# A hybrid mLSTM and GDN block: odd heads' first phases one piece later, one decay load moved, and the gate's sigmoid in the mLSTM's own stage

## The chip, the core and the metric

The kernel runs on one core of a Trainium2 chip. The metric is the device time of one execution in microseconds (us). A core has five engines with a queue each: TensorE (PE) for matmuls, VectorE (DVE), ScalarE (ACT), GpSimd (POOL) and SyncE (SP). Each engine works its queue in order. SP, POOL and ACT also issue DMA transfers.

## The reference

One layer of a bidirectional encoder, for 256 tokens of width 2048 in float32. A first matrix product of c gives shifts, scales and gates (ada); a second projects the normed input h to the inputs of two branches and of their merge:

```python
proj = h @ w_in
# branch A, mLSTM, 4 heads: q, k of 256, v and output gate o of 512
h_a = bidirectional(mlstm_chunkwise, (q_a, k_a, v_a), ...)
y_a = (jax.nn.sigmoid(a_o) * rms_norm(h_a)) @ w_branch_a
# branch B, GDN (gated delta rule), 16 heads of 128
o_b = bidirectional(gated_delta_chunkwise, (q_b, k_b, v_b), ...)
y_b = (rms_norm(o_b) * jax.nn.silu(b_z)) @ w_branch_b
x = x + gate_m * ((g_a * y_a + g_b * y_b) @ w_out)
# then a SwiGLU feed-forward of width 5632, and a final RMSNorm
```

The gated delta rule needs, for each head, the inverse of a unit triangular matrix; the mLSTM needs row sums of its decayed scores for its denominator. The output gate is the sigmoid of a_o.

## The kernel before

**Matmuls.** The large products are made of float32 operands split in two (fp32r): the weights come as tiles of 1 MB (`raw`), ScalarE copies half a tile to `wh` (L182, L209) and VectorE subtracts to get `wl` (L184, L211); TensorE then makes three matmuls for each block. Half a tile's matmuls are a *piece*: in `tjob` 12 matmuls over 512 columns (L230 to L232), in `fjob` 24 matmuls over 256 columns (L187 to L189). The pool of `raw` has three buffers, and wh and wl have three each. The ada rows, also 1 MB each, share the `raw` buffers; VectorE sums each of them (L111).

**Jobs.** A weight tile is named after its job. b8_2 is the third projection of GDN head 8 (j = 0, 1, 2: k, q and v; the v part ends in `vf`, a silu on ScalarE at L337). z0 to z3 are the gates of the four groups of GDN heads. v, o, a and m jobs (o = output gate; ma and mb = merge gates; a = q and k of the mLSTM) make up the list `fills`: work that nothing near it waits for. `fill(n)` puts n pieces of it into the program.

**GDN.** 16 heads in 4 groups of 4. `gdn_phase1(h)` has two steps. The first makes the decay scans, and on TensorE the transposes of vf (`vps`, L601) and the sums of squares (L603). The second makes square roots (L611), products k k and q k (`ks`, L630), the matrices mi and mb, and ends with POOL's DMAs: four stores to `inst_d` (L651), the load of the decays of head h + 2 (`decay_load`, a memset at L312 and a DMA at L313), and the load of a part of `uu` (L658). `gdn_invert(g)` then solves for the group's inverses on VectorE; it begins with a memset (L687) that waits for the last load of uu, and yields to a fill piece every few steps. `gdn_phase2(g, p)` works off two heads p of group g; its last step (`px`, L829) transposes the result, ScalarE scales it into `obt` (L833) and stores it to `ob_d` (L834).

**What sets the order.** The program is written out in one order for all engines. While the two heads of a pair run phase 2, `stream(h0)` puts in the b jobs of two heads of the next group (6 pieces for each head), and then fill pieces; each of these pieces counts down the list `todo`. An entry `[n, h]` runs the next step of head h's phase 1 when n more pieces have been put in. After a head's last b piece the entries `[2, h]` and `[4, h]` are added. Then a group's last pair goes on taking pieces until its second head is done, the job z of the next group is put ahead of the fills, and the group's solve begins.

**The mLSTM's head.** Behind the last px the GDN's memory is given back, and the mLSTM's heads 0 and 1 go on: `pden` (L950, row sums by matmuls of one column), `dn` (L952, its absolute value, in the memory that the GDN's had), the loads of the four parts of ob_d (`o4`, L1066, two buffers), `ph` (L966, the numerators, in the four PSUM buffers that pden also uses), their eviction into hs with dn as the scale (L968, L969), and a square with sum (L970). `o_split` cuts o4 into `obh` (L1070) and `obl` (L1071), the operands of the branch product `yb`. The output gate `sgo` comes back from o_d by POOL's DMA (L939). What is left of `fills` is put in by fill(1), fill(2) and fill(1000) among these steps; the yb job is what follows.

Of the kernel before, what the change touches and what calls it, by code (L numbers as in the profile page):

```python
# [11 lines left out]
AF = mybir.ActivationFunctionType  # L12
# [9 lines left out]
NH_B, DK_B = 16, 128  # L22
# [3 lines left out]
GRP = 4  # L26
# [26 lines left out]
def hybrid_block(ctx: ExitStack, tc: tile.TileContext, xr, nfr, crow, pk_d, cst_d, ada2, ada4, win0, winb, wint, wba, wbb, wo, wgu, wd, out, dbg=None):  # L53
    nc = tc.nc
    V, S, G, PE = nc.vector, nc.scalar, nc.gpsimd, nc.tensor
# [228 lines left out]
    v_d = [tc.dram_tile([P, 2, 512], F32, name=f"v_d{h}") for h in range(NH_A)]  # L284
    o_d = [tc.dram_tile([P, 2, 512], F32, name=f"o_d{h}") for h in range(NH_A)]
# [24 lines left out]
    def decay_load(h):  # L310
        al = als[h] = fr.tile([P, 2, T + 8], F32, tag="al", bufs=2, name=f"al{h}")
        order(G.memset(al[:, :, 0:8], 0.0))  # L312
        order(G.dma_start(al[:, :, 8:], alpha_d[:, h].partition_broadcast(P)))  # L313
# [32 lines left out]
    def keep(dst, fn, name):  # L346

        def done(ps):
            ev = evp.tile([P, 2, 512], F32, tag="ev", bufs=2, name=f"ev_{name}")
            for t in range(2):  # L350
                S.activation(ev[:, t], ps[t], fn)
            S.dma_start(dst, ev)
        return done
# [21 lines left out]
    def a_vo(i, h):  # L375
        return tjob(
            f"{'vo'[i]}{h}", [wint[4 + 4 * i + h, u] for u in range(4)], hh, hl,
            keep((v_d, o_d)[i][h], (AF.Copy, AF.Sigmoid)[i], f"{'vo'[i]}{h}"),
        )

    def m_job(i, g):
# [201 lines left out]
    def gdn_phase1(h):  # L583
# [62 lines left out]
        g, hl_ = divmod(h, GRP)  # L646
# [5 lines left out]
                inst[4 * b : 4 * b + 4].rearrange("x j i -> j x i"), mi[32 * b : 32 * b + 32, :, 32 * b : 32 * b + 32]  # L652
            ), b)

        final = hl_ == GRP - 1
        if h + 2 < NH_B and not final:
            decay_load(h + 2)
        order(G.dma_start(uus[g][16 * hl_ : 16 * hl_ + 16], inst))  # L658
        if h + 2 < NH_B and final:
            decay_load(h + 2)  # L660

        cc = ccs[h % NB]

# [211 lines left out]
    def stream(h0):  # L875

        todo = []

        def piece():

            for q in list(todo):
                q[0] -= 1
                if not q[0]:
                    todo.remove(q)
                    next(heads1[q[1]])

        for h in range(h0, min(h0 + 2, NH_B)):
            for j in range(3):
                for _ in b_job(h, j):
                    piece()  # L890
                    yield True
            todo += [[2, h], [4, h]]
        while todo:
            fill(1)
            piece()
            yield True
        while True:
            fill(1)
            yield True
# [3 lines left out]
    def mlstm(h):  # L903
# [34 lines left out]
        so = ml.tile([P, 2, DV_A], F32, tag="so", bufs=2, name=f"sgo{h}")  # L938
# [21 lines left out]
        for t in range(2):  # L960
            pn = []
            for d in range(2):
                ph = gps(f"ph{h}_{t}_{d}")
                terms = src[d, t]
                for i, (w, s) in enumerate(terms):
                    PE.matmul(ph, w, vt[:, s], start=i == 0, stop=i == len(terms) - 1)  # L966
                pn.append(ph)
            S.activation(hs[:, t], pn[0], AF.Copy, scale=dn[:, t, 0:1])  # L968
            V.scalar_tensor_tensor(hs[:, t], pn[1], dn[:, t, 1:2], hs[:, t], ALU.mult, ALU.add)  # L969
            S.activation(sq, hs[:, t], AF.Square, accum_out=ss[:, t : t + 1])  # L970
            yield
        S.activation(ss, ss, AF.Sqrt, bias=epsc, scale=1.0 / DV_A)
        V.reciprocal(ss, ss)
        for t in range(2):
# [2 lines left out]
        for e2 in range(2):  # L977
            px = gps(f"pxa{h}_{e2}")
            for e in range(2):
                f = 2 * e2 + e  # L980
# [25 lines left out]
    def invert(g):  # L1006
        gen = gdn_invert(g)
        next(gen)
        fill(4 if g else 6)
        for _ in gen:  # L1010
            fill(1)

    invert(0)
# [365 lines left out]
    for j in range(FB // 4):  # L1379
# [4 lines left out]
        for e2 in range(2):  # L1384
            px = gps(f"pxf{j}_{e2}")
            for e in range(2):
                f = 2 * e2 + e
# [154 lines left out]
```

## Time and profile before

| what | value |
| --- | --- |
| three runs | 2049.5, 2056.79 and 2057.14 us, median 2056.79 us |
| the profiled execution | 2056.26 us |
| its span, from the first instruction to the last | 2054.3 us |
| mean granted TensorE clock | 0.992 |
| GDN stage (from the second group's b jobs to the last px) | 323 to 983 us of the span |
| head of the mLSTM | 983 to about 1115 us |

All times in the text are microseconds from the start of the span. A row of the timeline gives the start, the duration, the engine, the line of the kernel, the operation, the tile written, the tiles read, and in brackets how long the engine stood idle ahead of it and what it waited for; xN is a group of N instructions. A row of the windows view gives a stretch's length, the busy time of each engine in it with the number of instructions, the granted TensorE clock as a part of 1, the share of DMA in use, and GB/s. A matmul of float32 that isn't split stands as two records.

### The profile page before, as it was taken

How to read it: one execution, taken by the hardware profiler on the slowest of the kernel's cores; microseconds unless marked ns; L12 is line 12 of the kernel's file. 1: busy time of each engine (PE TensorE's matmuls, PEld its weight loads, DVE VectorE, ACT ScalarE, POOL GpSimd, SP SyncE). 2: the span in 40 equal slices, each digit the busy share in tenths (PEclk: the TensorE clock that was granted, in tenths of full speed). 3: DMA queues.
4: the chain of work that ended last, by engine and by line, in shares of the span. 5: the costliest groups of instructions: out<-in, count | busy, mean ns of one | idle time of the engine just before them, and what ended most of it. 6: DMA issues, size and time to landing. Idle time of an engine off the chain costs nothing.

```text
span 2054.3 us, 27025 instructions
## 1 busy us (share of the span) xinstructions
PE 2017.2 (98%) x10386; PEld 1698.6 (83%) x10386; DVE 1397.7 (68%) x2062; ACT 1027.4 (50%) x1541; POOL 116.6 (6%) x211
## 2 busy tenths in 40 slices
PE   8999999999999999999999999999999999999998
PEld 6878789988997888889787888788888888878886
DVE  5778877877888788866577778756556554555554
ACT  3146647765675667455534444644444444444443
POOL 0001210111011010100100000200000000000000
PEclk9999999999999999999999999999999999999999
DMA  9986666656666666686776877466666665555553
GB/s 400 420 332 209 195 224 227 220 165 212 226 199 221 245 205 226 205 288 260 260 269 254 309 292 289 163 236 237 237 226 234 254 226 187 193 194 196 193 192 136
DMA packets 78962, 485.64 MB, mean 236 GB/s; under 512 B 10585, under 2 KB 15969, under 8 KB 24433
## 3 DMA queue, kind: packets, MB, share of 16 engines
q1 hardware_dynamic: 63216, 450.69, 60.5%
q0 software_dynamic: 8160, 17.88, 3.9%
q10 hardware_dynamic: 7458, 15.36, 2.0%
q8 instruction: 81, 1.33, 0.3%
q14 instruction: 47, 0.39, 0.1%
HBM read 467.07 MB, written 16.82 MB: 236 GB/s over the span
## 4 chain that ended last, share of the span: by engine, by line
PE 86%; DMA 6%; DVE 5%; ACT 1%; issue 1%; POOL 0%; ACTq 0%; SPq 0%; DVEq 0%; POOLq 0%
PE acc_gt L230 4%; PE acc_gt L232 4%; PE acc_gt L231 4%; PE acc_up L232 4%; PE acc_up L231 4%; PE acc_up L230 4%; PE acc_d L230 4%; PE acc_d L232 4%; PE acc_d L231 4%; DMA ra<-ada 3%; PE acc_o L232 3%; PE acc_o L230 3%; PE acc_o L231 3%; PE acc_b L187 2%; PE acc_b L188 2%; PE acc_b L189 2%
## 5 line engine op out<-in xcount | busy, mean ns | idle before, releaser
L211 DVE TENSOR_TENSOR wl_d<-raw_d,wh_d 128x1024 fp32r<-128x1024 f32 x88 | 107.9, 1226 | 119.9 <-ACT wh_d L209 119.9
L211 DVE TENSOR_TENSOR wl_up<-raw_up,wh_up 128x1024 fp32r<-128x1024 f32 x88 | 107.8, 1226 | 111.9 <-ACT wh_up L209 111.9
L211 DVE TENSOR_TENSOR wl_gt<-raw_gt,wh_gt 128x1024 fp32r<-128x1024 f32 x88 | 108.6, 1234 | 89.1 <-ACT wh_gt L209 89.1
L187 PE MATMUL acc_b<-hh,wh_b 128*128 128x256 f32 x576 | 164.7, 286 | 0.0
L209 ACT ACTIVATE wh_d<-raw_d 128x1024 fp32r<-128x1024 f32 x88 | 93.3, 1061 | 139.0 <-PE acc_d L231 134.0
L189 PE MATMUL acc_b<-hh,wl_b 128*128 128x256 f32 x576 | 160.8, 279 | 0.0
L188 PE MATMUL acc_b<-hl,wh_b 128*128 128x256 f32 x576 | 159.6, 277 | 0.0
L209 ACT ACTIVATE wh_gt<-raw_gt 128x1024 fp32r<-128x1024 f32 x88 | 93.3, 1060 | 128.7 <-PE acc_gt L231 77.3
L111 DVE SCALAR_TENSOR_TENSOR ada<-ada,crow 128x2048 f32<-128x2048 f32 x64 | 146.2, 2284 | 10.8 <-DMA ada<-ada 10.8
L209 ACT ACTIVATE wh_up<-raw_up 128x1024 fp32r<-128x1024 f32 x88 | 93.2, 1060 | 118.0 <-PE acc_up L231 84.2
L230 PE MATMUL acc_gt<-wh_gt,hfh 128*128 128x512 f32 x352 | 139.2, 395 | 0.1
L231 PE MATMUL acc_gt<-wh_gt,hfl 128*128 128x512 f32 x352 | 138.3, 393 | 0.0
L232 PE MATMUL acc_gt<-wl_gt,hfh 128*128 128x512 f32 x352 | 137.5, 391 | 0.0
L230 PE MATMUL acc_up<-wh_up,hfh 128*128 128x512 f32 x352 | 136.9, 389 | 0.0
L231 PE MATMUL acc_up<-wh_up,hfl 128*128 128x512 f32 x352 | 136.9, 389 | 0.0
L232 PE MATMUL acc_up<-wl_up,hfh 128*128 128x512 f32 x352 | 136.9, 389 | 0.0
L230 PE MATMUL acc_d<-wh_d,ffh 128*128 128x512 f32 x344 | 134.3, 391 | 0.0
L231 PE MATMUL acc_d<-wh_d,ffl 128*128 128x512 f32 x344 | 134.3, 390 | 0.0
L232 PE MATMUL acc_d<-wl_d,ffh 128*128 128x512 f32 x344 | 133.9, 389 | 0.0
L557 PE MATMUL first<-x,raw 128*128 128x256 f32 x512 | 115.9, 386 | 6.4 <-ACT x L551 6.4
L557 PEld LDWEIGHTS first<-x,raw 128*128 128x128 f32 x512 | 97.3, 192 | 25.1 <-ACT x L551 12.0
L187 PEld LDWEIGHTS acc_b<-hh,wh_b 128*128 128x128 f32 x576 | 108.4, 188 | 1.2 <-issue 0.9
(374 smaller groups left out, 5262.6 us busy)
## 6 DMA issues: line engine op xcount, KB each, us to landing
ada<-ada SPq DMA_DIRECT2D x64, 1024.0 KB, 4.9
raw_gt<-wgu SPq DMA_DIRECT2D x44, 1024.0 KB, 4.9
raw_up<-wgu SPq DMA_DIRECT2D x44, 1024.0 KB, 4.9
raw_d<-wd SPq DMA_DIRECT2D x44, 1024.0 KB, 4.8
raw_b<-winb SPq DMA_DIRECT2D x36, 1024.0 KB, 5.0
ra<-ada SPq DMA_DIRECT2D x32, 1025.0 KB, 15.3
raw<-win SPq DMA_DIRECT2D x16, 1024.0 KB, 14.5
raw_z<-wint SPq DMA_DIRECT2D x16, 1024.0 KB, 5.5
```

Of the source, the lines that this page charges most:

```text
L111: order(V.scalar_tensor_tensor(raw, raw, 1.0, row_c[:, :D], ALU.mult, ALU.mult, accum_out=mod[:, c : c + 1]), room[0][3] > 1)
L187: PE.matmul(o, wh[:, k], hh[:, kk], start=kk == 0, stop=False)
L188: PE.matmul(o, wh[:, k], hl[:, kk], start=False, stop=False)
L189: PE.matmul(o, wl[:, k], hh[:, kk], start=False, stop=kk == KB - 1)
L209: order(S.activation(wh, raws[u][:, k0 : k0 + 2], AF.Copy), early)
L211: order(V.tensor_tensor(wl, raws[u][:, k0 : k0 + 2], wh.bitcast(F32), ALU.subtract), early)
L230: order(PE.matmul(ps[t], xh[:, kk, c], wh[:, k], start=kk == 0, stop=False), early and steps > 1)
L231: PE.matmul(ps[t], xl[:, kk, c], wh[:, k], start=False, stop=False)
L232: PE.matmul(ps[t], xh[:, kk, c], wl[:, k], start=False, stop=kk == last)
L557: PE.matmul(first[o], raw[:, o], x[:, b], start=b == 0 and o % 2 == 0, stop=b == KB - 1 and o % 2 == 1)
```

## The change

There are three parts.

1. For odd heads the two steps of phase 1 come 3 and 5 pieces after the last b piece, in place of 2 and 4.
2. The decay load for the head 4g + 5 isn't made at the end of head 4g + 3's phase 1, but in `invert`, when the solve of group g has made its first step.
3. The output gate's job evicts a_o as it is (Copy), and the sigmoid is taken in `mlstm`, in place on `so` (the tile sgo, 128x1024), ahead of the square root of ss.

```diff
@@ a_vo
-            keep((v_d, o_d)[i][h], (AF.Copy, AF.Sigmoid)[i], f"{'vo'[i]}{h}"),
+            keep((v_d, o_d)[i][h], AF.Copy, f"{'vo'[i]}{h}"),
@@ gdn_phase1
-        final = hl_ == GRP - 1
-        if h + 2 < NH_B and not final:
+        if h + 2 < NH_B and hl_ < GRP - 1:
             decay_load(h + 2)
         order(G.dma_start(uus[g][16 * hl_ : 16 * hl_ + 16], inst))
-        if h + 2 < NH_B and final:
-            decay_load(h + 2)
@@ stream
-            todo += [[2, h], [4, h]]
+            todo += [[2 + h % 2, h], [4 + h % 2, h]]
@@ mlstm
+        S.activation(so, so, AF.Sigmoid)
         S.activation(ss, ss, AF.Sqrt, bias=epsc, scale=1.0 / DV_A)
@@ invert
-        for _ in gen:
+        for i, _ in enumerate(gen):
+            if not i and g < 3:
+                decay_load(4 * g + 5)
             fill(1)
```

In the order of instructions this shows as follows. A number behind a name is the instance of the tile. First VectorE's queue at the start of the solve of group 2: `wl_z2_u_k` is a cut of a weight tile of job z2, `dec12` the decay scans of head 12, and `uu2` the matrix that the solve works on. Before:

```order
L645 STREAM_TRANSPOSE mi11_5727<-mb11_5728 128x256
L211 TENSOR_TENSOR wl_z2_0_0_5771<-raw_z2_0_5768,wh_z2_0_0_5770 128x1024
L211 TENSOR_TENSOR wl_z2_0_2_5793<-raw_z2_0_5768,wh_z2_0_2_5792 128x1024
L211 TENSOR_TENSOR wl_z2_1_0_5811<-raw_z2_1_5808,wh_z2_1_0_5810 128x1024
...
L211 TENSOR_TENSOR wl_z2_1_2_5827<-raw_z2_1_5808,wh_z2_1_2_5826 128x1024
L593 SCALAR_TENSOR_TENSOR dec12_6598<-al12_5494,cst_75 128x128
L687 MEMSET uu2_4728 64x32
...
L211 TENSOR_TENSOR wl_z2_2_0_5854<-raw_z2_2_5851,wh_z2_2_0_5853 128x1024
```

And after:

```order
L645 STREAM_TRANSPOSE mi11_5811<-mb11_5812 128x256
L211 TENSOR_TENSOR wl_z2_1_2_5898<-raw_z2_1_5879,wh_z2_1_2_5897 128x1024
...
L593 SCALAR_TENSOR_TENSOR dec12_6672<-al12_5567,cst_75 128x128
L211 TENSOR_TENSOR wl_z2_2_0_5928<-raw_z2_2_5925,wh_z2_2_0_5927 128x1024
L211 TENSOR_TENSOR wl_z2_2_2_5950<-raw_z2_2_5925,wh_z2_2_2_5949 128x1024
L684 MEMSET uu2_4796 64x32
...
L211 TENSOR_TENSOR wl_z2_3_0_5974<-raw_z2_3_5971,wh_z2_3_0_5973 128x1024
```

Head 11's last products (mi11) now stand behind three cuts of z2, and the memset of the solve behind six cuts in place of four.

Second, ScalarE's queue ahead of the solve of group 3: `vf15` is head 15's silu, `ev_o2` the eviction of the output gate's job, `nn15` the square root of head 15, and `obt10`, `obt11` the results of heads 10 and 11. Before:

```order
L337 ACTIVATE vf15_7296<-cv15_2_7505 128x256
L351 ACT_TABLE_LOAD
L351 ACTIVATE ev_o2_7578<-acc_o2_0_6217 128x512
L351 ACTIVATE ev_o2_7578<-acc_o2_1_6218 128x512
L611 ACT_TABLE_LOAD
L611 ACTIVATE nn15_7662<-vps15_7589,epsc_83 128x4
...
L621 ACTIVATE vv15_7668<-vps15_7589,nn15_7662 128x128
L833 ACTIVATE obt10_7699<-px_2_1_7531,pk_74 128x256
L833 ACTIVATE obt11_7702<-px_2_1_7531,pk_74 128x256
...
L209 ACTIVATE wh_z3_0_0_7711<-raw_z3_0_7709 128x1024
```

And after:

```order
L337 ACTIVATE vf15_7433<-cv15_2_7642 128x256
...
L847 ACT_TABLE_LOAD
L847 ACTIVATE so2_1_7696<-so2_1_7696,epsc_83 128x4
L182 ACTIVATE wh_a2_3_8_7832<-raw_a2_3_7792 128x1024
L209 ACTIVATE wh_z3_0_0_7903<-raw_z3_0_7901 128x1024
...
L611 ACTIVATE nn15_7864<-vps15_7784,epsc_83 128x4
...
L209 ACTIVATE wh_z3_0_2_7925<-raw_z3_0_7901 128x1024
L830 ACTIVATE obt10_7826<-px_2_1_7681,pk_74 128x256
```

The first two cuts of z3 moved ahead of obt10, and the eviction of o2 with its table loads stands elsewhere.

Third, ScalarE's queue around the end of the GDN: `ma3` is the last fill job, `obt14`, `obt15` the last results of the GDN, `dn0`, `hs0` and `sqh0` steps of mLSTM head 0, and `wh_yb0_u_k` cuts of the branch product. Before:

```order
L209 ACTIVATE wh_ma3_2_2_9228<-raw_ma3_2_9210 128x1024
L833 ACTIVATE obt14_9133<-px_3_1_9041,pk_74 128x256
L833 ACTIVATE obt15_9136<-px_3_1_9041,pk_74 128x256
L834 DMA ob_d3_117<-obt14_9133 128x256
L834 DMA ob_d3_117<-obt15_9136 128x256
L209 ACTIVATE wh_ma3_3_0_9288<-raw_ma3_3_9286 128x1024
L952 ACTIVATE dn0_9185<-pden0_9178 128x4
L952 ACTIVATE dn1_9202<-pden1_9195 128x4
L209 ACTIVATE wh_ma3_3_2_9304<-raw_ma3_3_9286 128x1024
L1070 ACTIVATE obh_9153<-o4_0_9155 128x1024
L209 ACTIVATE wh_yb0_0_0_9349<-raw_yb0_0_9347 128x1024
```

And after:

```order
L209 ACTIVATE wh_yb0_0_2_9368<-raw_yb0_0_9350 128x1024
L351 ACT_TABLE_LOAD
L351 ACTIVATE ev_ma3_9216<-acc_ma3_0_9011 128x512
...
L830 ACTIVATE obt14_9224<-px_3_1_9151,pk_74 128x256
...
L209 ACTIVATE wh_yb0_1_0_9386<-raw_yb0_1_9384 128x1024
L831 DMA ob_d3_117<-obt15_9227 128x256
L950 ACTIVATE dn0_9260<-pden0_9253 128x4
...
L1071 ACTIVATE obh_9244<-o4_0_9246 128x1024
...
L970 ACTIVATE sgo0_9251<-sgo0_9251 128x1024
```

The cuts of ma3, and with them its matmuls, moved ahead of obt14; cuts of yb0 stand around it instead, and the sigmoid of sgo0 is new.

## The prediction

> **What bounds the kernel now.** I read the page first (the span, the busy times and the chain that ended last), then a table of busy time by stretches of the part that the change touches, and last the timelines of the engines at each place where TensorE waits there.
>
> ```profile
> span 2054.3 us, 27025 instructions
> PE 2017.2 (98%) x10386; PEld 1698.6 (83%) x10386; DVE 1397.7 (68%) x2062; ACT 1027.4 (50%) x1541; POOL 116.6 (6%) x211
> PE 86%; DMA 6%; DVE 5%; ACT 1%; issue 1%; POOL 0%; ACTq 0%; SPq 0%; DVEq 0%; POOLq 0%
> ```
>
> TensorE sets the time: 2017.2 of 2054.3 us busy, and 86% of the chain. The change adds and removes no matmul, so it can give only what TensorE loses by waiting, or by running at a lower granted clock, near the moved steps. All idle time of the whole run is 37.1 us (2054.3 - 2017.2), and 0.5% of the time is 10.3 us, about what a measurement of this kernel can tell from no change.
>
> Stretches of the GDN stage and of the mLSTM's head, from the windows view (length, busy PE, PEld, DVE, ACT, POOL, then granted clock, DMA share and GB/s):
>
> ```profile
> 382.00:441.00 59.00, 58.42 (x446) 54.44 (x445) 47.59 (x96) 41.39 (x86) 6.92 (x14) 1.00 0.63 201
> 540.00:558.50 18.50, 16.07 (x142) 15.88 (x141) 17.00 (x35) 11.69 (x33) 3.48 (x7) 1.00 0.83 275
> 558.50:566.00 7.50, 7.47 (x37) 7.47 (x38) 4.02 (x15) 4.00 (x8) 0.00 (x0) 0.54 0.39 165
> 570.00:630.00 60.00, 58.88 (x457) 55.17 (x457) 51.63 (x106) 42.98 (x88) 6.92 (x14) 1.00 0.69 228
> 641.00:650.00 9.00, 7.05 (x31) 5.47 (x30) 7.22 (x20) 2.48 (x3) 0.00 (x0) 1.00 0.43 139
> 758.00:819.00 61.00, 59.67 (x474) 56.10 (x472) 50.62 (x107) 43.84 (x90) 6.16 (x12) 1.00 0.65 225
> 819.00:828.00 9.00, 6.89 (x23) 5.48 (x24) 6.21 (x11) 6.12 (x12) 2.68 (x5) 0.81 0.38 110
> 986.00:1002.00 16.00, 16.00 (x61) 10.81 (x62) 5.90 (x11) 4.62 (x7) 3.35 (x5) 0.89 0.84 304
> 1002.00:1052.00 50.00, 49.98 (x220) 39.46 (x219) 35.14 (x44) 29.06 (x43) 5.98 (x10) 1.00 0.77 281
> ```
>
> Three places lose time: 540 to 566 (idle, then a clock of 0.54 for 7.5 us), 641 to 650, and 819 to 828 (idle, then a lower clock). The head of the mLSTM (986 to 1052) loses nothing to waiting: 65.98 of 66 us busy.
>
> **Part 1, odd heads one piece later.** I take its places in order of time.
>
> Head 9's phase 1, in the first pair of group 1's phase 2:
>
> ```profile
> 558.53 0.65 PE L601 MATMUL vps<-cst,vf 128*128 128x128 f32 x2 [2.46 <-ACT vf L337]
> 557.11 1.06 ACT L182 ACTIVATE wh_a<-raw_a 128x1024 fp32r<-128x1024 f32 x1 [4.02 <-DMA raw_a<-winb]
> 558.08 0.40 ACT L337 ACTIVATE vf<-cv 128x256 f32<-128x256 f32 x1
> ```
>
> The transposes of vf wait 2.46 us; vf stands on ScalarE right behind a cut of a fill's weights that itself waited 4.02 us for its load. Behind the stall the clock is 0.54 for 7.5 us, which is (1 - 0.54) x 7.5 = 3.4 us of lost work: 5.9 us in all. The change sets one more fill piece ahead of these transposes, which would cover the 2.46. But that piece needs a weight tile too, and the load that came late stays: at the start of this pair a fill tile is still half used, before and after (of job a1_1 before, a1_2 after), so that one of the three raw buffers is held. I take half of it, 3.0 us gained; the ends are 0 (the late load stalls the fill itself) and 5.9.
>
> The same hold can be counted at the other pairs in SP's order of loads. Before it is also there in the pair from 570 (a1_3) and not in the pairs from 382 and 758; after it is gone from the pair at 570 and comes to the other two (mb1_0 and a2_1). The idle time by the rows: 1.12 us with the hold (570:630), 0.58 (382:441) and 1.33 (758:819) without it. So it is worth little by these rows: 0.6 gained (0 to 1.1) and 1.0 lost at each of the two new places (0 to 2.46 each, the stall that the hold at 558 had part in), 2.0 lost.
>
> The solve of group 2:
>
> ```profile
> 644.51 0.50 PE L232 MATMUL acc_z<-wl_z,hh 128*128 128x512 f32 x1 [1.95 <-DVE wl_z L211]
> 642.40 0.19 DVE L692 TENSOR_TENSOR utmp<-uu 64x30 f32<-64x30 f32 x1 [5.48 <-issue]
> 643.25 1.21 DVE L211 TENSOR_TENSOR wl_z<-raw_z,wh_z 128x1024 fp32r<-128x1024 f32 x1
> 636.78 0.52 POOL L658 DMA_DIRECT2D uu<-inst_d x1 [3.71 <-DMA inst_d<-mi]
> ```
>
> VectorE stands 5.48 us in the solve's first step, waiting for the load of uu that POOL issued at 636.78, with a cut of z's weights queued behind it; TensorE waits 1.95 us for that cut. In the new order two more cuts of z stand ahead of the memset (six in place of four), so the piece that was late is cut before VectorE enters the wait. I take 1.95 us gained, at the least 1.0 (the load of uu also starts a piece later).
>
> The solve of group 3:
>
> ```profile
> 821.11 0.53 PE L230 MATMUL acc_z<-wh_z,hh 128*128 128x512 f32 x1 [2.51 <-ACT wh_z L209]
> 811.51 1.28 ACT L351 ACT_TABLE_LOAD   x1
> 812.80 1.09 ACT L351 ACTIVATE ev_o<-acc_o 128x512 f32<-128x512 f32 x2
> 813.91 1.28 ACT L611 ACT_TABLE_LOAD   x1
> 818.64 0.84 ACT L833 ACTIVATE obt<-px,pk 128x256 f32<-128x256 f32 x2 [1.00 <-PE px L829]
> 820.00 1.06 ACT L209 ACTIVATE wh_z<-raw_z 128x1024 fp32r<-128x1024 f32 x1 [0.52 <-ACT obt L833]
> ```
>
> The first cut of z3 stands on ScalarE behind obt, which waits for TensorE's px: 2.51 us idle, and then (1 - 0.81) x 9 = 1.7 us of clock. After, that cut stands ahead of obt and of vv, and two of the four table loads of that stretch are gone with the sigmoid of part 3. What is late next is the second cut, for which the first piece of z3 is cover. I take the whole 4.2 us; the least is 2.5, if the clock drops there anyway.
>
> **Part 2, the decay load.** POOL's order is the same instruction by instruction: before and after, the memset and the load of al stand between the last load of uu and the solve's first store. SP's and VectorE's queues don't hold it. Nothing moves; 0.
>
> **Part 3, the sigmoid, and with part 1 the head of the mLSTM.** Each odd head takes one more fill piece while the GDN runs, so the fills end sooner. Before, five pieces of ma3 stand behind px (TensorE's last step of GDN), between it and yb0; after, all of them stand ahead of px. What they covered:
>
> ```profile
> 982.67 0.44 PE px L829 x4
> 985.88 2.57 PE pden L950 x24
> 993.13 0.23 PE acc_ma L231
> 995.65 7.87 PE ph L966 x18
> 1003.55 2.84 PE ph L966 x6
> ```
>
> ```profile
> 983.93 1.57 ACTq L834 DMA_DIRECT2D ob_d<-obt  x2
> 990.25 0.24 ACT L952 ACTIVATE dn<-pden 128x4 f32<-128x4 f32 x2 [3.52 <-DMA ob_d<-obt]
> 990.80 1.51 POOL L1066 DMA_DIRECT2D o<-ob_d  x2 [63.38 <-ACT dn L952]
> 998.05 1.06 ACT L1070 ACTIVATE obh<-o 128x1024 fp32r<-128x1024 f32 x1 [4.28 <-DMA o<-ob_d]
> 999.14 1.23 DVE L1071 TENSOR_TENSOR obl<-o,obh 128x1024 fp32r<-128x1024 f32 x1 [4.12 <-ACT obh L1070]
> DMA to landing us min/median/max: 1.7/3.0/5.8
> o<-ob_d POOLq DMA_DIRECT2D x4, 512.0 KB, 6.3
> sgo<-o_d POOLq DMA_DIRECT2D x2, 512.0 KB, 10.9
> ```
>
> (The last three are landing times: of the stores of obt, and of the two kinds of loads in the stretch 980 to 1012.) px ends at 983.11. The chain from there to obl, which yb0's second matmul needs, ends at 999.14 + 1.23 = 1000.37, 17.3 us later: the store of obt lands, then dn (its memory was the GDN's), then the load of o4, then its cut. TensorE has work without ob_d for 2.57 + 7.87 + 2.84 = 13.3 us; the five pieces added 5 x 12 x 0.23 = 13.8. Without them it waits 17.3 - 13.3 = 4.0 us, part of it already before the third group of ph, whose PSUM buffer dn must free. In the new order ev_ma's pair (1.09, as ev_o's) stands ahead of obt, and a cut (1.06, as that of z) between obt and its second store: up to 2.1 more. The store landed at its slowest here, the median is 2.8 us less, and the load of o4 took 998.05 - 990.80 = 7.2 against a median of 6.3: up to 3.7 less. I take 4.0; the ends are 2.4 and 6.1.
>
> The sigmoid of so itself: four of 128x1024, 1.06 us each by the row of obh, which has that shape, and table loads around it (1.28 each). The first stands ahead of obh's third and fourth part and of the cut of yb0's fourth piece, and waits for sgo: issued behind o4, it lands 10.9 us later, some 20 us behind px. Sigmoid, hs, a table load, the square root, a square, two obh and the cut are then about 7 us, so that cut is ready near 27, where TensorE wants it at 17.3 + 3 x 2.75 = 25.6. With the second pair of table loads ahead of a later cut I take 2.0 us lost; 0 if the extra wait for obl pushes TensorE's need back by as much, 4.0 if both count in full.
>
> Clock: in 986:1002 it is (1 - 0.89) x 16 = 1.8 us down, behind pden's thin matmuls, and this is paid before as well. A wait right behind them may bring as much again: I take 1.0 (0 to 1.7). The Trainium skill, in "TensorE: Matmul & The Clock Gate", section "What's actually happening", has the clock halved after one idle window of about 3.4 us, the windows running free of the work. By that rule 2.57 us of thin matmuls and 4 us of waiting would bring the whole 1.7, and the sum below would be 0.7 us higher; the stall of 1.95 us at 644 with a clock of 1.00 behind it, and those of 2.46 and 2.51 with half clock, agree with it.
>
> **The sum.** The profiled execution took 2056.26 us (span 2054.3 and 2.0 around it), 0.5 under the median of the runs (2056.79). Gains 3.0 + 0.6 + 1.95 + 4.2 = 9.8; losses 2.0 + 4.0 + 2.0 + 1.0 = 9.0. Net 0.8 less: 2055.5, or 2056.0 from the median; I say 2055.5.
>
> **The rivals.**
>
> - *The gains stay, the head of the mLSTM is covered.* If the store lands in its median time and o4 soon after, and sgo doesn't hold the queue, only 2.4 us are lost there; with the whole 5.9 at head 9 this is -12.7 + 2.0 + 2.4 = -8.3, and -10 or so without the new holds: 2046 to 2048. For it: DMA has fewer weight loads to carry when TensorE stands. Against: two cuts are now in ScalarE's queue around the store. Chance 0.2, half of it beyond 0.5%.
> - *The starved head.* Slower: with no fill left behind px, TensorE stands twice, before ph's third group and before yb0, and sgo's late landing then holds the cuts of yb0. Price 6.1 + 4.0 + 1.7 = 11.8, and with nothing gained at head 9 and 4.9 at the two new holds -6.8 + 4.9 + 11.8 = +9.9: 2066. It decides if obl ends over 20 us behind px. For it: the chain's 17.3 us are measured, and its cover is gone. Against: this takes the dear end of each term. Chance 0.2, half of it beyond 0.5%.
> - *The change does nothing.* The decay load stays where it is, and the stalls only pass from the moved steps to their neighbours: 2056.3, within the forecast's range. Chance 0.1.
>
> The forecast itself has 0.5, with ends near 2049 and 2061, and a few hundredths of it reach past the lower bound where no buffer is held. The range that holds 8 in 10 goes from 2046 to 2066. Faster by over 0.5%: 0.13; within: 0.77; slower: 0.10.
>
> **What would show it.** Right: no idle time over 1 us ahead of the first matmul of z3 and the third group's cuts of z2, a shorter one ahead of head 9's vps; the same POOL order with al's load right behind uu's; and new idle time of 4 to 8 us between px and yb0's last piece, released by dn and obl. Wrong: TensorE over 99% busy from px to yb0's end, which would take 7 us off; or a stall of over 3 us with half clock in the pairs that now hold a buffer.

## The result and the profile after

The changed kernel takes 2076.14 us (median; 2073.38 to 2080.32) against 2053.9 us of the kernel before on the same chip: a ratio of 1.0116, with a 95% interval of 1.01 to 1.0131. It is 22 us slower. The forecast was 2055.5, and the measured time lies outside its range of 2046 to 2066. The profiled execution has a span of 2075.0 us, 20.7 more than that of before.

The page of the changed kernel, first its span and the busy time of TensorE, then the shares of the chain that ended last:

```profile
span 2075.0 us, 27027 instructions
PE 2024.0 (98%) x10386; PEld 1702.4 (82%) x10386; DVE 1397.6 (67%) x2062; ACT 1030.1 (50%) x1544; POOL 118.0 (6%) x211
PE 77%; DMA 10%; DVE 8%; issue 2%; ACT 2%; POOL 1%; SPq 0%; POOLq 0%; ACTq 0%; DVEq 0%
```

TensorE has the same 10386 matmuls. Its share of the chain fell from 86% to 77%, and DMA and VectorE took most of what it lost. Idle time went from 37.1 to 51.0 us, and busy time rose by 6.8 us; the lower clock in three of the stretches below makes 6.3 of that.

To see where, here are both kernels in the same stretches (columns as in the prediction: length, busy PE, PEld, DVE, ACT, POOL, clock, DMA share, GB/s). What a stretch loses is its length less PE's busy time, and (1 - clock) times its length. First before:

```profile
382.00:445.00 63.00, 62.42 (x465) 57.62 (x464) 51.59 (x108) 43.49 (x93) 6.99 (x15) 1.00 0.63 206
445.00:505.00 60.00, 60.00 (x302) 50.71 (x300) 46.47 (x91) 32.63 (x41) 9.87 (x19) 1.00 0.64 209
505.00:635.00 130.00, 126.16 (x973) 118.94 (x973) 107.89 (x209) 89.45 (x184) 12.59 (x25) 0.97 0.65 214
635.00:700.00 65.00, 62.61 (x285) 51.07 (x284) 48.52 (x92) 32.35 (x39) 7.78 (x15) 1.00 0.65 223
970.00:1060.00 90.00, 89.97 (x409) 70.99 (x408) 55.56 (x82) 43.88 (x69) 9.86 (x16) 0.98 0.76 276
```

and after:

```profile
382.00:445.00 63.00, 59.47 (x439) 55.07 (x438) 48.98 (x94) 40.19 (x83) 6.92 (x14) 0.97 0.60 193
445.00:505.00 60.00, 57.06 (x245) 45.04 (x244) 46.87 (x104) 28.11 (x37) 7.94 (x15) 1.00 0.61 207
505.00:635.00 130.00, 121.50 (x946) 116.09 (x945) 96.52 (x174) 80.83 (x158) 8.93 (x18) 0.95 0.64 223
635.00:700.00 65.00, 61.89 (x301) 50.20 (x300) 50.87 (x108) 38.07 (x62) 9.21 (x18) 1.00 0.55 188
970.00:1060.00 90.00, 85.36 (x438) 68.04 (x437) 53.45 (x78) 53.03 (x89) 9.33 (x15) 0.96 0.73 257
```

| stretch | lost before (idle + clock) | lost after | difference |
| --- | --- | --- | --- |
| 382 to 445, second pair of group 0 | 0.6 + 0 | 3.5 + 1.9 | +4.8 |
| 445 to 505, solve of group 1 | 0 | 2.9 | +2.9 |
| 505 to 635, pairs of group 1 | 3.8 + 3.9 | 8.5 + 6.5 | +7.3 |
| 635 to 700, solve of group 2 | 2.4 | 3.1 | +0.7 |
| 970 to 1060, around px and yb0 | 0.0 + 1.8 | 4.6 + 3.6 | +6.4 |

These five make 22.1 us; between 700 and 970 the changed kernel wins 1.6, so that 20.5 of the 20.7 us are placed. (As the later kernel lags, the same stretch doesn't hold quite the same work. And the clock stands with two places, so that its part can be 0.7 us off in a stretch of 130 us and 1.4 in one of 270; that the sum fits to 0.2 us is in part luck.) Four places show what happens.

Second pair of group 0, SP's, VectorE's and TensorE's rows of the timeline:

```profile
392.16 0.33 SPq L129 DMA_DIRECT2D ada<-ada  x1
400.50 2.29 DVE L111 SCALAR_TENSOR_TENSOR ada<-ada,crow 128x2048 f32<-128x2048 f32 x1 [3.47 <-DMA ada<-ada]
403.11 0.68 DVE L769 TENSOR_TENSOR pt<-p,cst 128x512 f32<-128x512 f32 x1
403.85 0.32 PE L780 MATMUL p<-X,pt 128*128 128x64 f32 x1 [2.75 <-DVE pt L769]
```

VectorE waits 3.47 us for an ada row, with pt behind it in its queue; TensorE waits 2.75 us for pt, and half clock follows. That row was issued 2.8 us behind a decay load (389.39) and took 8.3 us to land.

Solve of group 1:

```profile
468.74 0.20 DVE L689 TENSOR_TENSOR utmp<-uu 64x30 f32<-64x30 f32 x1 [5.79 <-DMA uu<-inst_d]
469.35 1.21 DVE L211 TENSOR_TENSOR wl_z<-raw_z,wh_z 128x1024 fp32r<-128x1024 f32 x1
470.61 0.50 PE L232 MATMUL acc_z<-wl_z,hh 128*128 128x512 f32 x1 [1.14 <-DVE wl_z L211]
463.45 0.51 POOL L657 DMA_DIRECT2D uu<-inst_d  x1 [5.22 <-DMA inst_d<-mi]
```

This is the wait of the solve of group 2 in the kernel before (5.48 us on VectorE there), now in groups 1 and 2: POOL waits 5.22 us for the stores of inst_d, then issues the load of uu, and VectorE stands 5.79 us with cuts of z behind it. TensorE waits 1.14 us here and 1.80 us once more at 483.86.

First pair of group 1, the kernel's largest new stall (POOL, SP, ACT and PE rows, then the time to landing of raw_a, and a second stall in the same stretch):

```profile
561.82 0.73 POOL L313 DMA_DIRECT2D al<-alpha_d  x1
562.72 0.33 SPq L178 DMA_DIRECT2D raw_a<-winb  x1
572.13 2.00 ACT L182 ACTIVATE wh_a<-raw_a 128x1024 fp32r<-128x1024 f32 x2 [4.82 <-DMA raw_a<-winb]
573.24 0.58 PE L187 MATMUL acc_a<-hh,wh_a 128*128 128x256 f32 x1 [4.17 <-ACT wh_a L182]
raw_a<-winb SPq DMA_DIRECT2D x1, 1024.0 KB, 9.3
619.80 0.58 PE L601 MATMUL vps<-cst,vf 128*128 128x128 f32 x2 [2.49 <-ACT vf L337]
```

A weight load of a fill job is issued 0.9 us behind a decay load, and lands after 9.3 us. TensorE waits 4.17 us for the fill piece itself, the one that the change put ahead of head 9's transposes. The second stall, 2.49 us at the transposes of a head of the next pair, has half clock behind it too. vf stands there on ScalarE behind work that waits for VectorE, and no wait of over 0.4 us for a load stands just ahead of it; its cause was not settled.

Behind px:

```profile
1018.92 0.24 ACT L950 ACTIVATE dn<-pden 128x4 f32<-128x4 f32 x2 [4.69 <-DMA ob_d<-obt]
1019.15 9.69 PE L964 MATMUL ph<-vt,mdec 128*128 128x512 f32 x18 [2.17 <-ACT dn L950]
1036.73 1.06 ACT L1071 ACTIVATE obh<-o 128x1024 fp32r<-128x1024 f32 x1 [1.23 <-DMA o<-ob_d]
1037.69 1.99 ACT L209 ACTIVATE wh_yb<-raw_yb 128x1024 fp32r<-128x1024 f32 x2
1038.78 0.50 PE L230 MATMUL acc_yb<-wh_yb,obh 128*128 128x512 f32 x1 [1.76 <-ACT wh_yb L209]
```

TensorE waits 2.17 us for dn ahead of ph's third group, and 1.76 us for the cut of yb0's fourth piece, which stands on ScalarE behind a part of obh that waits for its load.

### The profile page after: what moved, and what is told of

The parts are those of the page before. It is cut to its first block, busy times and chain, and to the rows that moved or that the text cites. A ratio compares the mean times of both kernels' runs of the same rounds, so it can differ in the third digit from the quotient of the medians.

```text
span 2075.0 us, 27027 instructions
## 1 busy us (share of the span) xinstructions
PE 2024.0 (98%) x10386; PEld 1702.4 (82%) x10386; DVE 1397.6 (67%) x2062; ACT 1030.1 (50%) x1544; POOL 118.0 (6%) x211
## 4 chain that ended last, share of the span: by engine, by line
PE 77%; DMA 10%; DVE 8%; issue 2%; ACT 2%; POOL 1%; SPq 0%; POOLq 0%; ACTq 0%; DVEq 0%
PE acc_gt L230 4%; PE acc_gt L232 4%; PE acc_gt L231 4%; PE acc_up L232 4%; PE acc_up L231 4%; PE acc_up L230 4%; PE acc_d L230 4%; PE acc_d L232 4%; PE acc_d L231 4%; DMA ra<-ada 3%; PE acc_o L232 2%; PE acc_o L231 2%; PE acc_o L230 2%; PE acc_b L187 2%; PE acc_b L189 2%
## 5 line engine op out<-in xcount | busy, mean ns | idle before, releaser
L209 ACT ACTIVATE wh_gt<-raw_gt 128x1024 fp32r<-128x1024 f32 x88 | 93.3, 1060 | 128.6 <-PE acc_gt L231 77.2
L209 ACT ACTIVATE wh_up<-raw_up 128x1024 fp32r<-128x1024 f32 x88 | 93.2, 1060 | 118.1 <-PE acc_up L231 84.3
```

Of the source, the lines that this page charges most:

```text
L209: order(S.activation(wh, raws[u][:, k0 : k0 + 2], AF.Copy), early)
```

## The experiments

Ratios are to the kernel before, run beside each on the same chip, with 95% intervals. The theories that the expectations name: A, the stagger of the odd heads by one piece makes the whole loss, by a wait for uu (A1), by a buffer held half used (A2) and, later, by decay loads ahead of weight loads (A3); B, the sigmoids make a part of it; C, any later phase 1 costs.

**The stagger alone.**

```diff
-            todo += [[2, h], [4, h]]
+            todo += [[2 + h % 2, h], [4 + h % 2, h]]
```

> The stagger of the odd heads alone; the decay load and the sigmoid stay as before. Theory A (the stagger of one piece makes the whole loss: a fill tile half used at the start of other pairs, the load of uu later against the solve, and no fill left behind the last px): 2071 to 2078 us, as the changed kernel, with TensorE idle by about 3 us near 404, near 573, in the solves of groups 1 and 2, and by 5 to 8 us behind px. Theory B (the new sigmoids and their table loads in the mLSTM's head make a part of it): 2062 to 2069 us, with the idle time behind px under 4 us.

Measured: 2071.69 us, ratio 1.009 (1.0064 to 1.0115): 18.6 us over before, where the changed kernel is 22. The two stretches that matter:

```profile
505.00:635.00 130.00, 120.79 (x939) 115.30 (x938) 95.80 (x171) 80.03 (x157) 8.97 (x18) 0.95 0.66 221
970.00:1060.00 90.00, 88.30 (x463) 70.68 (x463) 56.49 (x79) 47.30 (x87) 9.36 (x15) 0.98 0.74 266
```

The losses up to 700 us are those of the changed kernel to about 2 us; around px it loses 1.7 + 1.8 us, not 8.2, and not the 5 to 8 us of idle time that theory A has there. So the stagger makes nearly all. That it doesn't make the part behind px is read from the two traces: the intervals of the two times overlap.

**Everything but the stagger.** Parts 2 and 3 of the change, as in the diff of the change.

> The moved decay load and the moved sigmoid without the stagger. The order of POOL, SP and TensorE is then that of before, instruction by instruction, and ScalarE's and VectorE's differ only around the sigmoids. Theory A: 2050 to 2057 us, the same as before within 0.3%; a gain of 2 to 4 us if the first cut of z3 now stands ahead of obt, which the order shows. Theory B: 2060 us or more, with new idle time behind px.

Measured: 2054.02 us, ratio 1.0008 (0.9991 to 1.0024), no difference that can be told. Behind px:

```profile
970.00:1060.00 90.00, 87.77 (x370) 67.61 (x369) 54.98 (x78) 47.33 (x63) 9.89 (x16) 0.96 0.73 254
```

2.2 us of idle time and 3.6 of clock are lost there, 4.0 more than before. In this execution the stalls of groups 2 and 3 were smaller by as much, so the total stays. The moved decay load was not run by itself; that it does nothing follows from its unmoved place on POOL (behind the load of uu at 669.36 comes the decay load at 669.91, as at 636.78 and 637.33 before).

**An even stagger of three heads.** Heads 5, 7 and 9 two pieces later.

```diff
-            todo += [[2, h], [4, h]]
+            late = 2 * (h % 2) * (h < 10)
+            todo += [[2 + late, h], [4 + late, h]]
```

> Heads 5, 7 and 9 two pieces later, the later odd heads as before: six pieces in all, as many as the change takes, but an even number at each pair, so that the fill tiles are half used where they were before. Nothing else is changed. Theory A: no stall near 404, and those near 573 to 620 are gone or under 2 us; the loss behind px stays, 5 to 8 us: 2058 to 2065 us. Rival C (a later phase 1 costs by itself, through the later stores of inst_d and the later load of uu): the stalls of the stage from 382 to 700 stay or grow, 2070 us or more.

Measured: 2060.27 us, ratio 1.0037 (1.0023 to 1.0051). The time is what theory A says, and too short for C, but not for A's reasons: 3.5 us are lost behind px in place of 5 to 8, and a stall of the changed kernel's kind stands later, at another fill's weight load.

```profile
643.36 0.50 PE L230 MATMUL acc_ma<-wh_ma,hh 128*128 128x512 f32 x1 [3.56 <-ACT wh_ma L209]
raw_ma<-wint SPq DMA_DIRECT2D x1, 1024.0 KB, 10.0
630.71 0.73 POOL L313 DMA_DIRECT2D al<-alpha_d  x1
```

That load was issued at 632.24, again behind a decay load, by 1.5 us (630.71), and took 10.0 us. This put the suspicion on the decay loads.

**No fill behind px, no head moved.**

```diff
-    last = (0, 1, 2, 1, 2, 2, 1, 1, 3, 0)
+    last = (0, 1, 2, 1, 2, 2, 2, 2, 4, 0)
```

> Only the tail: the last group's pairs take 16 pieces each in place of 13 (the row of fill pieces for groups 0 to 2 used for group 3 too), so that no fill piece is left behind the last px, as in the changed kernel; no head is moved. Theory A: nothing changes before 887 us, and 5 to 8 us are lost between px and the third piece of yb0, while the last group's phase 2 itself may gain 1 to 2 us with more cover: 2057 to 2063 us. If the loss behind px in the changed kernel came from its sigmoids, this one loses under 3 us there: 2052 to 2057 us.

Measured: 2054.49 us, ratio 1.0008 (0.9991 to 1.0025).

```profile
970.00:1060.00 90.00, 86.94 (x392) 67.19 (x391) 55.86 (x82) 44.54 (x71) 9.89 (x16) 0.98 0.76 272
```

3.1 us are idle behind px in place of none, among them the wait for dn, but this execution idles 3.2 us less between 635 and 970, most of it ahead of 887, where the edit moves nothing. By the time of the runs the missing fill alone costs nothing that can be told. Theory A's 5 to 8 us fall.

**All cuts of z ahead of the solve.**

```diff
-            order(V.tensor_tensor(wl, ..., ALU.subtract), early)
+            order(V.tensor_tensor(wl, ..., ALU.subtract), early or name[0] == "z")
...
-        fill(4 if g else 6)
+        fill(8 if g else 6)
...
-        fill(8)
+        fill(4 if g else 8)
```

> The changed kernel, with all eight cuts of z ahead of the memset that begins the solve on VectorE (the cuts of z are put in program order, eight fill pieces ahead of the memset and four fewer behind the solve). Theory A1 (VectorE enters the solve before the load of uu has landed, and cuts are queued behind it): the stalls at 471 and 484 and at 677 and 690, 6.5 us together, go, and the time is 14 to 17 us over before, where the changed kernel is 20 to 23. Rival (those stalls come from VectorE's load in the solve itself, not from the wait for uu): the stalls at 484 and 690 stay, and no more than 3 us are won, 18 to 21 over before.

Measured: 2068.8 us, ratio 1.0063 (1.0042 to 1.0085): 15.4 us over before, as theory A1 has it.

```profile
468.44 0.20 DVE L689 TENSOR_TENSOR utmp<-uu 64x30 f32<-64x30 f32 x1 [0.40 <-DMA uu<-inst_d]
445.00:505.00 60.00, 60.00 (x278) 49.22 (x277) 48.20 (x103) 31.82 (x41) 7.94 (x15) 1.00 0.66 222
```

The load of uu lands when it did, but VectorE cuts in the meantime and waits 0.40 us; TensorE loses nothing in the solve of group 1 any more, at 484 neither. The stall at 573 stays (4.16 us).

**Even pairs.** One more fill piece at each pair's end.

```diff
                 while 4 * g + 2 * p + 5 not in heads:
                     next(pieces)
+                fill(1)
...
-        fill(8)
+        fill(6 if g else 8)
```

> The changed kernel with one more fill piece at the end of each pair of groups 0 to 2, so that a pair takes an even number as before and no tile is half used where none was before; two fewer are put in behind each solve, so that as many are used up before the last px. Theory A2 (a tile half used at the start of a pair, which holds one of three buffers, makes loads late): the stall at 404 goes, and those near 573 and 620 fall under 2 us each: 8 to 14 us over before. Rival C (it is the lateness of phase 1 itself): 18 us or more over before, with stalls of 2 us and more in the same stages.

Measured: 2075.69 us, ratio 1.0098 (1.0076 to 1.012): nothing won in all, which is the time of rival C and not of A2. The view is split:

```profile
382.00:445.00 63.00, 61.50 (x456) 56.60 (x455) 49.60 (x95) 44.23 (x86) 6.93 (x14) 1.00 0.65 215
402.04 2.29 DVE L111 SCALAR_TENSOR_TENSOR ada<-ada,crow 128x2048 f32<-128x2048 f32 x1 [1.31 <-DMA ada<-ada]
571.54 2.00 ACT L182 ACTIVATE wh_a<-raw_a 128x1024 fp32r<-128x1024 f32 x2 [5.62 <-DMA raw_a<-winb]
raw_a<-winb SPq DMA_DIRECT2D x1, 1024.0 KB, 10.2
```

Near 404 the wait for the ada row fell from 3.47 to 1.31 us and the stretch loses 1.5 us in place of 5.4: there the held buffer has a part. It isn't the cause by itself: in this order the ada row is also issued later behind the decay load, 4.6 us in place of 2.8, and the next runs take the same stall away with the buffer still held. The stall at 573 is as before or larger, behind a load of 10.2 us that was issued 0.9 us behind a decay load. Theory A2 falls for that place.

**The decay loads left out, in both kernels.**

```diff
     def decay_load(h):
-        al = als[h] = fr.tile([P, 2, T + 8], F32, tag="al", bufs=2, name=f"al{h}")
+        if h > 3:
+            als[h] = kept[h % 2]
+            return
+        al = als[h] = kept[h % 2] = fr.tile([P, 2, T + 8], F32, tag="al", bufs=2, name=f"al{h}")
```

> The changed kernel without the decay loads of heads 4 to 15: these heads use the decays of heads 2 and 3, so that 12 loads of 256 KB by POOL are left out. Theory A3 (POOL's burst of inst_d stores and of this load, which now falls on the loads of weights, makes these take 9 us in place of 5): the stalls near 573 and 620 go, 8 to 14 us over before. If the burst has no part, 18 to 22 us over before as the changed kernel.

> The kernel before without the decay loads of heads 4 to 15, in the same way; the pair of the run just before it. Theory A3: 1 to 6 us faster than before (its stall of 2.5 us with half clock at 558 goes, if that load was late for the same reason). Otherwise the same as before within 1 us. What counts is the distance of the two: under 12 us by theory A3, 18 to 22 without.

Measured: the changed kernel 2059.24 us, ratio 1.0027 (1.0014 to 1.004), so 5.8 us over before, less than the 8 to 14 expected; the kernel before 2045.49 us, ratio 0.9956 (0.9939 to 0.9973), so 8.0 us under, more than the 1 to 6 expected. The second pair of group 0 with its ada row, the pairs of group 1, and the load that took 9.3 us, in the changed kernel without decay loads:

```profile
382.00:445.00 63.00, 61.93 (x458) 56.79 (x457) 51.19 (x102) 42.59 (x88) 5.36 (x10) 1.00 0.60 209
397.45 2.29 DVE L111 SCALAR_TENSOR_TENSOR ada<-ada,crow 128x2048 f32<-128x2048 f32 x1 [0.45 <-DMA ada<-ada]
505.00:635.00 130.00, 127.78 (x1016) 121.13 (x1015) 109.19 (x200) 90.97 (x184) 8.47 (x16) 1.00 0.67 236
raw_a<-winb SPq DMA_DIRECT2D x1, 1024.0 KB, 5.1
```

and that stretch of the kernel before without them:

```profile
505.00:635.00 130.00, 128.03 (x991) 119.67 (x991) 109.36 (x211) 90.34 (x185) 10.76 (x20) 1.00 0.62 220
```

The same load now lands in 5.1 us, the stalls at 573 and 620 are gone, and the stretch loses 2.2 us in place of 15.0 (2.0 in place of 7.7 in the kernel before). Near 404 the ada row, issued at 392.13, lands in 5.3 us in place of 8.3, and the pair loses 1.1 us in place of 5.4, though one of its buffers is held as before. The decay loads cost the kernel before 8 us and the changed one 16. The two stay 13.8 us apart, over the 12 that theory A3 set: the decay loads make 8.5 of the 22 us between the two, the largest single cause, and not the only one.

The change didn't make more such collisions. From 320 to 960 us each kernel has six loads of 1 MB on SP that are issued within 3 us behind a decay load. They took 5.8 to 10.8 us before and 7.0 to 9.5 after; the loads issued over 5 us behind one have medians of 5.0 and 4.9. What the change moved is which loads are hit, and whether TensorE waits for them.

**The decays of both directions in one row of 2 KB.** The same bytes in half as many rows, 128 of 2 KB in place of 256 of 1 KB, in both kernels; nothing is left out.

```diff
-    alpha_d = tc.dram_tile([2, NH_B, T], F32, name="alpha_d")
+    alpha_d = tc.dram_tile([NH_B, 2, T], F32, name="alpha_d")
...
-        al = als[h] = fr.tile([P, 2, T + 8], F32, tag="al", bufs=2, name=f"al{h}")
-        order(G.memset(al[:, :, 0:8], 0.0))
-        order(G.dma_start(al[:, :, 8:], alpha_d[:, h].partition_broadcast(P)))
+        al = als[h] = fr.tile([P, 2 * T + 16], F32, tag="al", bufs=2, name=f"al{h}")
+        order(G.memset(al[:, 0:16], 0.0))
+        order(G.dma_start(al[:, 16:], alpha_d[h].rearrange("d t -> (d t)").partition_broadcast(P)))
...
-            G.dma_start(alpha_d.rearrange("d h t -> (d h) t"), s2[32:64])
+            for d in range(2):
+                G.dma_start(alpha_d[:, d], s2[32 + 16 * d : 48 + 16 * d])
...
-        af, ab = al[:, 0, 8:], al[:, 1, 8:]
+        af, ab = al[:, 16 : 16 + T], al[:, 16 + T :]
```

> The kernel before with each head's decays for both directions next to each other in memory, so that the decay load writes one row of 2 KB to each partition in place of two of 1 KB: half as many packets, the same bytes, the same order on every engine; nothing is left out. If the number of packets is what makes this load slow and delays the weight loads behind it: the load lands in 4 to 5 us in place of 6 to 7, and 1 to 5 us are won over before. If the bytes are what counts: 0, within 1 us.

> The changed kernel with the same edit. By the number of packets: the weight loads that now fall behind this load take 7 us in place of 9, and the kernel is 10 to 16 us over before in place of 22. By the bytes: 20 to 24 us over before.

Measured: the kernel before with this edit takes 2046.33 us, ratio 0.9969 (0.9958 to 0.9979); it beats both kernels, by 6 us, a little more than the 1 to 5 expected, and by about 30. The changed kernel with it takes 2064.19, ratio 1.0059 (1.0043 to 1.0074): 11.7 us over before in place of 22. The landing times of all decay loads of the kernel before with the edit (the median was 6.5 without it), its stretch of group 1, and from the two pages the packets of POOL's queue, without the edit and with it (number, MB, and the share of the DMA engines' time that they took):

```profile
DMA to landing us min/median/max: 3.5/5.2/8.1
505.00:635.00 130.00, 127.47 (x985) 119.50 (x985) 109.64 (x211) 88.91 (x183) 13.27 (x28) 0.99 0.63 221
q0 software_dynamic: 8160, 17.88, 3.9%
q0 software_dynamic: 8192, 17.88, 3.3%
```

and that stretch of the changed kernel with it:

```profile
505.00:635.00 130.00, 124.38 (x981) 118.36 (x980) 105.42 (x188) 85.85 (x177) 10.22 (x22) 0.97 0.66 229
```

So the length of the rows counts, not the bytes alone. The number of packets does not: the expectations take half as many for granted, but the profile counts no fewer, 80 for each decay load without the edit (7200 in all are left where 12 loads are left out), and with it 32 more in all; each takes less time. Where the weight load is issued right behind, as in the changed kernel, it still takes 8.7 us in place of 9.3, not the 7 expected, and a stall of 3.58 us at 567 stays; what its trace shows as won is the stalls near 404 and 620. The Trainium skill, in "DMA: Bandwidth & Descriptors", section "Queues, rings and completion order", says that a DMA engine takes turns between the queues that have work for it, a packet at a time. Both pairs of runs agree with that in direction, if a packet that takes less time makes a shorter turn; no run here shows the turns themselves.

**Both mends together.** The rows of 2 KB and the cuts of z ahead of the solve, first on the kernel before and then on the changed one.

> The kernel before with the decays in rows of 2 KB and with all cuts of z ahead of the solve's memset. Theory A1 wins the stall of 2.1 us in the solve of group 2 and 0.6 behind it, and, since the cuts of z3 are in order too, perhaps a part of the 2.5 us at 821: 3 to 7 us faster than before with what the rows of 2 KB bring, 2047 to 2051 us.

> The changed kernel with both edits. If the wait for uu, the collision of loads and the sigmoids behind px are the whole loss, what is left is 6 to 8 us behind px and 3 to 5 near 404, less the 4 us won at 821: 4 to 10 us over before. If over 14 us stay, a part of the loss has another cause.

Measured: the kernel before 2058.84 us, ratio 1.0038 (1.0023 to 1.0052), the changed one 2055.37, ratio 1.0022 (1.001 to 1.0035). On the changed kernel the mends add up (2.9 us over before, under the 4 to 10 expected). On the kernel before, where 2047 to 2051 us were expected, the ordered cuts do harm: 12.5 us slower than with the 2 KB alone. In the solve of group 1 of this run's trace a cut of z now waits behind head 7's products, and in group 3 an ada row comes late:

```profile
443.67 0.50 PE L232 MATMUL acc_z<-wl_z,hh 128*128 128x512 f32 x1 [1.90 <-DVE wl_z L211]
887.87 2.29 DVE L111 SCALAR_TENSOR_TENSOR ada<-ada,crow 128x2048 f32<-128x2048 f32 x1 [3.30 <-DMA ada<-ada]
891.56 0.80 PE L232 MATMUL acc_mb<-wl_mb,hh 128*128 128x512 f32 x1 [3.05 <-DVE wl_mb L211]
```

These two places make a part of the 12.5 us; that the ordered cuts cause the second one is not shown. But the times show that a mend made for one order is no mend for another.

**The sigmoids of heads 0 and 1 at their eviction**, alone on the changed kernel and with both mends.

```diff
-            keep((v_d, o_d)[i][h], AF.Copy, f"{'vo'[i]}{h}"),
+            keep((v_d, o_d)[i][h], AF.Sigmoid if i and h < 2 else AF.Copy, f"{'vo'[i]}{h}"),
...
-        S.activation(so, so, AF.Sigmoid)
+        if h > 1:
+            S.activation(so, so, AF.Sigmoid)
```

> The changed kernel with the output gates of mLSTM heads 0 and 1 taken as before, at the eviction of their job; only heads 2 and 3 take the sigmoid in the mLSTM's stage. The order on TensorE, POOL and SP is that of the changed kernel. If the first two sigmoids with their table loads, ahead of obh and of the cuts of yb0 with no fill left, are the loss behind px: the excess from px to the first ya falls from 10.7 us to 5 to 6.5, and the kernel is 16 to 19 us over before in place of 22. If it is the missing fill pieces by themselves, the excess stays over 9 us.

> The changed kernel with all three edits: decays in rows of 2 KB, the cuts of z ahead of the solve's memset, the sigmoids of heads 0 and 1 at their eviction; the stagger of the odd heads stays. If these three causes are the loss, it is within 3 us of before (-3 to +1), of which the rows of 2 KB alone give before 6. If more than 4 us over before stay, a cause is missing.

Measured: 2073.77 us, ratio 1.0084 (1.0063 to 1.0105), and 2058.58 us, ratio 1.0027 (1.0015 to 1.0039). The first is 20.2 us over before by the medians; its interval reaches from 13 to 22, and so holds both what was expected and no gain at all. The second is 5.0 us over, where -3 to 1 was expected, and no better than without this edit (2.9): by its own terms a cause is missing. ScalarE and TensorE behind px, in the run with this edit alone:

```profile
1044.53 1.06 ACT L971 ACTIVATE sgo<-sgo 128x1024 f32<-128x1024 f32 x1 [6.68 <-DMA sgo<-o_d]
1046.58 0.50 PE L230 MATMUL acc_yb<-wh_yb,obh 128*128 128x512 f32 x1 [2.75 <-ACT wh_yb L209]
```

ScalarE, with less in its queue, comes sooner to the sigmoid of head 2, and stands 6.68 us for the load of its gate, with a cut of yb0 behind it. The run with all three mends shows the same wait (7.01 us at 1036.50), and so does the run of everything but the stagger (5.93 us at 1018.62). So taking the first two sigmoids away doesn't take the loss away: it passes to a sigmoid whose operand is still under way, in a queue that also feeds yb0. With the stagger alone, where the multiplication takes the gate on VectorE, the stretch loses 3.5 us; with the sigmoids 8.2 (changed) or 9.6 (this edit alone: 6.0 idle and 3.6 of clock). In the changed kernel's own trace no sigmoid up to 1060 waits over 0.5 us for its gate; there the parts of obh are what ScalarE waits for. How the sigmoids make the 4 to 6 us was not settled.

The traced execution of the run with all three mends took 2067.26 us, 8.7 over that run's median, with a stall of 5.07 us at 715 that no other trace has, so its other rows say little about the 5.0 us.

## Why the prediction was wrong, point by point

- **The bound: right.** The loss is all TensorE's waiting and clock; no engine became a new bound.
- **Head 9's phase 1, 3.0 us gained (0 to 5.9), and the pair behind it, 0.6 gained: wrong, and the largest part of the error.** The stretch that holds both lost 7.3 us more. The step that failed is "the load that came late stays", with 0 as its worst end. The prediction moved the transposes one piece on and left the loads where they stood against POOL's transfers. But head 8's and head 9's phase 1 move against SP's loads too. Before, the weight load of a1_3 was issued 3.5 us behind the decay load, 551.0 against 547.5, and took 6.0 us; after, it was issued 0.9 us behind, and took 9.3. So the piece that was to cover the transposes stalled itself, for 4.17 us in place of 2.46, with 3.4 us of clock behind it in both. The runs without decay loads show it: 12.8 of the 15.0 us in that stretch go, and the two kernels then lose the same there, 2.2 and 2.0. That the stall at 620 goes with them is shown; how it comes from them is not. The prediction treated the decay load as a matter of part 2 only, "Nothing moves; 0". That is right for its place on POOL, and part 1 moved it all the same in time.
- **The half used tiles, 2.0 lost at two new places, 0.6 gained at one: right in the places, wrong in the mechanism.** The pair at 382 lost 4.8 more, not 1.0; in the pair at 758 TensorE waits 1.31 us at 808, and the pair as a whole loses no more than before. At these three places TensorE waits for pt behind an ada row that was issued 1.3 to 2.8 us behind a decay load. The row that the price came from, 1.12 us in the pair from 570 before, is such a wait too (VectorE idle for 1.26 us at 584). Without decay loads 1.1 us are lost in the pair at 382 with the hold still there. So a hold sets when the ada row is issued, and the decay load makes it late.
- **The solve of group 2, 1.95 gained: wrong.** The prediction counted the cuts ahead of the memset, six in place of four. What counts is how much lies between head 11's products, which start the chain of stores and load, and the memset. That fell from four cuts to three (the order of the change shows it: mi11 now stands behind three of the six). So the wait on VectorE didn't go but grew, from 5.48 us (1.90 and 2.70 in the second and the fourth run above, with the order of before there) to 5.80, and TensorE's wait of 1.95 us became two, of 1.15 and 1.80. In group 1, for which the prediction had no term, it grew from 1.23 to 5.79 us and cost 2.9 us. The run with the cuts ahead of the solve shows it: the waits fall to 0.40 and 0.51 us, and neither solve loses anything.
- **The solve of group 3, 4.2 gained: right.** There is no stall left between px and z3: from 819 to 887 TensorE is busy 68.00 of 68.00 us at full clock, where 2.1 us of idle time and 1.7 of clock were lost before. 700 to 970 as a whole is 1.6 us better.
- **The decay load, 0: right** for the edit as such, by its order on POOL.
- **Behind px, 7.0 lost (2.4 to 11.8): right in size, 6.4, and wrong in its parts, so that the size is luck.** The missing fill was priced at 4.0 and loses 3.1 with nothing else changed, which that execution gave back elsewhere, and 1.7 with the stagger. The sigmoids, priced at 2.0, lose 4.0 alone and 4.7 on top of the stagger; the price was for a gate that comes late, and in the changed kernel's trace the sigmoids hardly wait for it.
- **The rivals.** The slower one placed the whole loss behind px and on the two held tiles, 2066. Its place was right for 11 us, but it left out the collision of loads and the wait for uu, and so ended 10 us short. No case had a new stall in the pairs of group 1 that is larger than the old one. Of the signs of being wrong, a stall of over 3 us with half clock in a pair that now holds a buffer, the nearest is the 2.75 us at 404; the larger stall came in the pair that held one before as well.
- **The clock.** Read in short windows, it took 1.7 us each behind the new stalls of 2.75 us at 404, 2.17 at 1019, 1.76 at 1039 and 1.35 at 929, and 3.4 each at 573 and 620; behind those of 1.80 us at 484 and 690 it didn't fall. So the price of 1.7 us, or twice that, is right, but the length of a stall doesn't tell whether it is paid. Nor do the stalls of 2.46 and 2.51 us before agree with the rule of one idle window, as the prediction says: both are shorter than the window that it quotes.

## What to carry to other kernels

A step moved by one place in the program moves all its transfers in time against the loads of other queues: for each, write down what is issued within a microsecond or two of it before and after, and price the collision from a pair of rows that shows it. When a step waits at the head of a queue, count the work between the start of its chain and the wait, not the work ahead of the wait. And a load in short rows is worth mending for its own sake: rows of twice the length for the decays won 6 us on one kernel and 10 on the other, while the ordered cuts of z, on top of them, won 8.8 us on the changed kernel and lost 12.5 on the kernel before.

## What the runs showed of the hardware

- Loads of 1 MB on SP that were issued 0.9, 0.9 and 1.5 us behind POOL's broadcast load of 256 KB landed after 9.3 (changed kernel), 10.2 (even pairs) and 10.0 us (two pieces later); the first of them took 5.1 with the broadcast loads left out.
- That broadcast load took 7.0 us (median of the changed kernel) in rows of 1 KB, and 5.5 in rows of 2 KB, for the same bytes and with no fewer packets counted.
- Half clock followed stalls of TensorE of 1.35 and 1.76 us and did not follow two of 1.80 us in the same trace (changed kernel).
